# First casts of raw weights inside attention's slots: kept at their program place on ScalarE's queue

## The chip, the cores and the metric

The kernel runs on 1 core of a Trainium2 chip. The metric is device time in microseconds (us) of one execution, as the median of 3 runs. An execution was also taken by the hardware profiler; all lines in fences below come from it. TensorE (PE) does matmuls and transposes, VectorE (DVE) and ScalarE (ACT) do elementwise work, GpSimd (POOL) and SyncE (SP) issue transfers (DMAs). Each engine works through a queue of its own in a fixed order; semaphores tell it when another engine's result is there.

## The reference

One layer of a diffusion backbone over 512 latent tokens of width 1024, with 256 context tokens. Everything is in float32.

```python
h = _rmsnorm(x, pre_g) * (1 + sc) + sh            # sh, sc, gt from silu(c) @ w_mod + b_mod
parts = split_in(h @ w_in)                        # b, c, x_in, z_a, q, k, v, z_b, g_a, g_b: 10 x 1024 columns
q, k = rope(parts[4]), rope(parts[5]); v = parts[6]
attn = neighbourhood_attention(q, k, v, k_ctx, v_ctx, rpb)   # 8 x 16 window + all context keys, one softmax
y_a = (silu(z_a) * b * dwconv3(c * x_in, conv_w, conv_b)) @ w_out_conv
y_b = (silu(z_b) * attn) @ w_out_attn
y = (sigmoid(g_a) * y_a + sigmoid(g_b) * y_b) @ w_o
return x + gt * _rmsnorm(y, post_g)
```

## The kernel before

**Numbers as pairs.** A float32 matrix is multiplied as two fp32r parts, high H and low L: three matmuls (H by H, H by L, L by H) stand for one. The helper `split` (L64) makes the pair: ScalarE casts the source to H (L67), VectorE subtracts H from the source to get L (L70). So each weight passes once through ScalarE and at least once through VectorE before TensorE can use it.

**Chunks of weights.** `Chunk` (L83) is 256 columns of a weight matrix: two transfers of 512 KB into `raw` tiles (L89; three such buffers), first and second half of the contraction. A plain chunk goes through `split` (L91): one 128x1024 cast and subtraction per half. A chunk for `pair` (L294) is multiplied in 2 by 2 blocks with sums of blocks. `first` (L98) makes four weights of it in this order: cast B11 (L101), add on VectorE (L102), cast T1 (L103), cast B21 (L104), add (L105), cast T2 (L106), then two more adds. `second` (L114) makes T3, T4, B22 (and B12 for queries and keys) when the chunk is used. `pair` uses the four of `first` in its first half (L299 to L304, in the order B11, B21, T1, T2) and the others in its second half (L309 to L312); between the halves it calls `chunk.more()` (L307), which loads the next chunk. Between the products, ScalarE copies results out of PSUM (L300, L303, L305, L311), and VectorE adds into them (L306, L314, L317); a product can start only when the bank that it writes has been read out. Three banks serve these products inside attention (L843).

**Attention's slots.** The loop at L850 goes over 64 slots: 8 pairs of heads, 2 heads, 4 blocks of 128 queries. A slot does, in program order: some steps of other projections, listed in `plan` (L219) and run by `step(items)` (L859); at a head's first block the product with the values for the head before, `gather` (L862, matmuls at L773); the scores of the block two slots ahead, `scores` (L864: matmuls L717 or L726, bias and row minimum on VectorE L733, exponentials on ScalarE L740 and L744, division L745 and L747); and in every second slot `turn2` (L871): TensorE transposes two blocks of probabilities (L754) and `split` makes the pair TH, TL of them (L67 and L70 again).

**Where the raw casts stand.** `load` (L134) issues a chunk's transfers when a step asks for it. Inside the loop, `behind` is a list: `load` puts the chunk's `ready` (L142), that is its `first` or `split`, into it, and the slot runs the list at its very end (L872), behind `turn2`. So the casts of a chunk stand in the program at the end of the slot in which it was asked for. Outside the loop `behind` is None, and `ready` runs at once.

**Who orders a queue.** Only the start of the kernel (L432) has its order written out by hand. Elsewhere the framework that compiles the program orders each engine's queue: it runs the program against its own estimates of when inputs are there, and among the instructions that it takes for ready it issues the one that stands earliest in the program. An instruction whose inputs it takes for ready early is so put ahead of others that stand before it in the program. `tc.keep_in_program_order` adds an edge from the instruction before it in the program, on the same engine: it is queued behind that one. The edge is order alone: no semaphore and no instruction is added. `split` has the argument `pinned` for this; before the change only the keys of `keys_queries` use it (L685, L689).

Of the kernel before, what the change touches and what calls it, by code (L numbers as in the profile page):

```python
# [27 lines left out]
def layer(ctx: ExitStack, tc, xp, ctxt, ctxT, cc, wmod, small, wfirst, win, wout, wo, rel, tab, out):  # L28
# [35 lines left out]
    def split(H, L, src, scale=None, pinned=False):  # L64

        if scale is None:
            cast = nc.scalar.copy(H, src)  # L67
            if pinned:
                tc.keep_in_program_order(cast)
            nc.vector.tensor_sub(L, src, H.bitcast(F32))  # L70
        else:
            nc.scalar.mul(H, src, scale)
            nc.vector.scalar_tensor_tensor(
                out=L, in0=src, scalar=scale, in1=H.bitcast(F32), op0=ALU.mult, op1=ALU.subtract
            )
# [4 lines left out]
    def wtile(shape):  # L80
        return wp.tile(shape, F32R, name="w", bufs=4)

    class Chunk:  # L83
# [7 lines left out]
        def split(self):  # L91
            t = [wtile([P, 4, 2, 256]) for _ in range(2)]
            for x, raw in zip(t, self.raws):
                split(x[:, :, 0], x[:, :, 1], raw)
            k = range(KT)
            return tuple([t[i // 4][:, i % 4, y] for i in k] for y in range(2)) + ([t[i // 4][:, i % 4] for i in k],)

        def first(self, keep=False):  # L98
            (b11, b12), (b21, b22) = self.b = [(r[:, :, :P], r[:, :, P:]) for r in self.raws]
            t, sums = (wtile([P, 2, 2, 4, P]) for _ in range(2))  # L100
            split(t[:, 0, 0], t[:, 0, 1], b11)  # L101
            nc.vector.tensor_add(b11, b11, b12)  # L102
            split(sums[:, 0, 0], sums[:, 0, 1], b11)  # L103
            split(t[:, 1, 0], t[:, 1, 1], b21)  # L104
            nc.vector.tensor_add(b11, b11, b22)  # L105
            split(sums[:, 1, 0], sums[:, 1, 1], b11)  # L106
            self.keep = keep
            if not keep:
                nc.vector.tensor_add(b12, b12, b22)
            nc.vector.tensor_add(b21, b21, b11)  # L110
            self.B = {"B11": t[:, 0], "B21": t[:, 1], "T1": sums[:, 0], "T2": sums[:, 1]}
            return self
# [13 lines left out]
    behind = None  # L126
# [167 lines left out]
    def pair(c1, c2, w=None):  # L294

        w = w or chunk().B
        a, b, e = (pj()[:, :256] for _ in range(3))
        first, second = slice(0, 256), slice(256, S)
        product(a, A11, w["B11"], True)  # L299
        nc.scalar.copy(c1[:, first], a)  # L300
        product(b, A12, w["B21"], True)
        product(e, blocks_h["X1"], w["T1"], True)
        nc.scalar.copy(c2[:, second], e)  # L303
        product(a, blocks_h["S2"], w["T2"], False)  # L304
        nc.scalar.copy(c2[:, first], a)  # L305
        nc.vector.tensor_add(c1[:, first], c1[:, first], b)  # L306
        chunk.more()  # L307
        yield
        product(b, A22, w["T4"], True)  # L309
        product(a, blocks_h["S3"], w["T3"], False)  # L310
        nc.scalar.copy(c1[:, second], a)  # L311
        product(e, blocks_h["S4"], w["B22"], False)  # L312
        for cols, x in ((second, c1[:, second]), (first, e)):
            nc.vector.scalar_tensor_tensor(  # L314
                out=c2[:, cols], in0=c2[:, cols], scalar=-1.0, in1=x, op0=ALU.mult, op1=ALU.subtract
            )
        nc.vector.tensor_add(c1[:, second], c1[:, second], b)  # L317
# [388 lines left out]
    def scores(p, h, b):  # L706
# [31 lines left out]
        if b % 2 == 0:  # L738
            z = aw.tile([P, 2], F32, name="z", bufs=4)
            nc.scalar.activation(pt, s, AF.Exp, bias=m, scale=-1.0, accum_out=z[:, 0:1])  # L740
            whole[:] = pt, z
        else:
            first, z = whole
            nc.scalar.activation(pt, s, AF.Exp, bias=m, scale=-1.0, accum_out=z[:, 1:2])  # L744
            nc.vector.reciprocal(z, z)  # L745
            for i, x in enumerate((first, pt)):
                nc.scalar.mul(x, x, z[:, i:i + 1])  # L747
# [99 lines left out]
    behind = []  # L847
    sums = block_sums()
    done = 0
    for i, (p, h, b) in enumerate(blocks):  # L850
# [23 lines left out]
        behind = []  # L874
    behind = None
# [73 lines left out]
    for j in range(KT):  # L949
# [30 lines left out]
        if j == 4:  # L980
            A11, S3 = operand("A11", hp, ("u2", "u3")), operand("S3", hp, ("a2", "a3"))
            for q in range(2):
                split(A11[q][:, 0], A11[q][:, 1], raws[q][:, :, h0])
                x = cv.tile([P, S], F32, name="tb").rearrange("p (k c) -> p k c", k=2)
# [96 lines left out]
    t = [hp.tile([P, 2, S], F32R, name=f"wB22{i}", tag=f"h{2 + i}") for i in range(4)]  # L1081
# [122 lines left out]
```

## Time and profile before

| | |
|---|---|
| median of 3 runs | 709.12 us (709.09 to 709.35) |
| the profiled execution's own time | 709.01 us |
| its span, first to last instruction | 707.2 us |
| mean granted TensorE clock | 0.997 |
| PE busy | 695.0 us, 98% of the span |
| DVE busy | 586.3 us, 83% |
| ACT busy | 436.5 us, 62% |

The profiled execution's time is 1.8 us more than its span, and 0.11 us below the median. Lines of a timeline read: start in us from the span's start, length, engine, source line, operation, what is written from what, shape, count, and in brackets how long the engine had been idle and what ended that. Attention's loop lies at about 137 to 500 us. A line of a helper such as L67 or L70 serves many callers; the tile (`w<-raw` for weights, `TH<-ps` for probabilities) tells them apart.

### The profile page before, as it was taken

The numbers are of one execution on the slowest core, as the hardware profiler recorded it, in microseconds if no ns is written. First come the engines' busy times: TensorE is split into PE (matmuls) and PEld (weight loads), VectorE is DVE, ScalarE is ACT, GpSimd is POOL, SyncE is SP. The second block draws the span as 40 slices with busy tenths as digits, with TensorE's granted clock in tenths as the row PEclk, the third lists the DMA queues.
The fourth block names the chain that finished last, engine by engine and source line by source line (L and its number), as shares of the span: only waits on it lengthen the run. The fifth ranks groups of instructions, "written<-read, shape, count | busy, mean of one in ns | idle before, by whom it ended". The sixth has DMA issues, their size and how long they took to land.

```text
span 707.2 us, 11426 instructions
## 1 busy us (share of the span) xinstructions
PE 695.0 (98%) x4196; PEld 618.0 (87%) x4196; DVE 586.3 (83%) x1114; ACT 436.5 (62%) x868; POOL 66.9 (9%) x110
## 2 busy tenths in 40 slices
PE   7999999999999999999999999999999999999996
PEld 4888888888889989898999999999898899988885
DVE  6979997668599989978898797999799676665996
ACT  6566632656577677775876766778693444442563
POOL 0000002230130310301302203000000000000000
PEclk9999999999999999999999999999999999999998
DMA  8996896564351563542635436313733233560013
GB/s 338 406 354 227 284 339 173 131 164 144 99 105 24 135 176 116 127 138 60 168 106 165 103 125 157 101 61 105 247 117 116 87 120 120 198 250 30 31 59 120
DMA packets 37466, 108.27 MB, mean 153 GB/s; under 512 B 5025, under 2 KB 5281, under 8 KB 37410
## 3 DMA queue, kind: packets, MB, share of 16 engines
q1 hardware_dynamic: 28946, 92.20, 37.8%
q0 software_dynamic: 8320, 15.21, 10.7%
q8 instruction: 33, 0.54, 0.3%
q14 instruction: 23, 0.19, 0.1%
q10 hardware_dynamic: 144, 0.13, 0.1%
HBM read 87.07 MB, written 5.24 MB: 131 GB/s over the span
## 4 chain that ended last, share of the span: by engine, by line
PE 91%; DVE 4%; DMA 2%; ACT 1%; issue 1%; SPq 0%; POOL 0%; DVEq 0%; ACTq 0%
PE ps L289 25%; PE ps L164 11%; PE ps L166 11%; PE ps L165 11%; PE ps L177 6%; PE ps L1008 5%; PE ps L773 4%; PE ps L754 3%; PE ps L182 3%; PE ps L717 3%; PE ps L196 2%; PE ps L424 2%; PE ps L428 2%; PE ps L425 2%; DMA fraw<-in_wfirst 1%; PE ps L726 1%
## 5 line engine op out<-in xcount | busy, mean ns | idle before, releaser
L67 ACT CAST w<-raw 128x512 fp32r<-128x512 f32 (+1 forms) x193 | 137.3, 733 | 95.9 <-PE ps L166 31.3
L70 DVE TENSOR_TENSOR w<-raw,w 128x512 fp32r<-128x512 f32 (+1 forms) x193 | 156.6, 824 | 42.3 <-ACT w L67 40.9
L289 PE MATMUL ps<-S,w 128*128 128x256 f32 x960 | 121.9, 283 | 0.0
L289 PEld LDWEIGHTS ps<-S,w 128*128 128x128 f32 x960 | 118.2, 192 | 0.1
L289 PE MATMUL ps<-h,w 128*128 128x256 f32 x720 | 94.0, 284 | 0.6 <-DVE tc L306 0.5
L289 PEld LDWEIGHTS ps<-h,w 128*128 128x128 f32 x720 | 89.9, 191 | 2.5 <-DVE tc L306 0.7
L164 PE MATMUL ps<-h,w 128*128 128x512 f32 x208 | 81.5, 392 | 0.0
L166 PE MATMUL ps<-h,w 128*128 128x512 f32 x208 | 81.2, 390 | 0.0
L165 PE MATMUL ps<-h,w 128*128 128x512 f32 x208 | 81.0, 390 | 0.0
L626 POOL DMA_DIRECT2D tc<-tb x32 | 28.8, 1175 | 286.7 <-DVE tc L624 197.7
L747 ACT ACTIVATE pt<-pt,z 128x512 f32<-128x512 f32 x64 | 43.0, 724 | 6.0 <-DVE z L745 5.9
L166 PEld LDWEIGHTS ps<-h,w 128*128 128x128 f32 x208 | 39.0, 188 | 8.3
L165 PEld LDWEIGHTS ps<-h,w 128*128 128x128 f32 x208 | 39.1, 188 | 8.0
L164 PEld LDWEIGHTS ps<-h,w 128*128 128x128 f32 x208 | 39.1, 188 | 7.9
L67 ACT CAST TH<-ps 128x512 fp32r<-128x512 f32 x64 | 35.8, 589 | 15.5 <-PE ps L754 15.5
L733 DVE CUSTOM_DVE_ANT_1 ps<-ps,bt 128x512 f32<-128x512 f32 x56 | 38.8, 693 | 6.8 <-PE ps L717 6.5
L70 DVE TENSOR_TENSOR TL<-ps,TH 128x512 fp32r<-128x512 f32 x64 | 42.2, 682 | 1.0 <-ACT TH L67 0.7
L754 PE MATMUL ps<-ident,pt 128*128 128x128 f32 x256 | 33.3, 273 | 0.0
L177 PE MATMUL ps<-w,h 128*128 128x512 f32 x128 | 32.3, 394 | 0.0
L754 PEld LDWEIGHTS ps<-ident,pt 128*128 128x128 f32 x256 | 29.2, 140 | 2.1 <-ACT pt L747 0.2
L740 ACT ACTIVATE pt<-ps,m 128x512 f32<-128x512 f32 x32 | 22.0, 688 | 12.5 <-DVE m L733 11.8
L773 PE MATMUL ps<-TH,V 128*128 128x256 f32 (+1 forms) x96 | 28.5, 319 | 0.2 <-ACT TH L67 0.2
(249 smaller groups left out, 1387.8 us busy)
## 6 DMA issues: line engine op xcount, KB each, us to landing
raw<-in_win SPq DMA_DIRECT2D x74, 512.0 KB, 4.4
wm<-in_wmod SPq DMA_DIRECT2D x34, 512.0 KB, 6.4
raw<-in_wout SPq DMA_DIRECT2D x16, 512.0 KB, 3.6
bt<-in_rel SPq DMA_DIRECT2D x16, 256.0 KB, 2.9
tc<-tb POOLq DMA_DIRECT2D x32, 128.0 KB, 3.6
B<-in_wo SPq DMA_DIRECT2D x8, 512.0 KB, 6.4
fraw<-in_wfirst SPq DMA_DIRECT2D x8, 384.0 KB, 8.6
qd<-qd POOLq DMA_DIRECT2D x24, 128.0 KB, 2.3
```

What stands on the lines that cost most here:

```text
L67: cast = nc.scalar.copy(H, src)
L70: nc.vector.tensor_sub(L, src, H.bitcast(F32))
L164: nc.tensor.matmul(ps, lhsT=H[k][:, cs], rhs=mH[k], start=k == 0, stop=False)
L165: nc.tensor.matmul(ps, lhsT=H[k][:, cs], rhs=mL[k], start=False, stop=False)
L166: nc.tensor.matmul(ps, lhsT=L[k][:, cs], rhs=mH[k], start=False, stop=k == KT - 1)
L177: nc.tensor.matmul(ps, lhsT=mH[k][:, ts], rhs=both[k].rearrange("p a c -> p (a c)"), start=k == 0, stop=False, skip_group_check=True,)
L289: nc.tensor.matmul(ps, lhsT=w[:, x, k], rhs=act[y][k], start=start and k + o == 0, stop=k == 3 and o == 2, skip_group_check=True,)
L733: nc.vector.tensor_tensor_reduce(out=s3, in0=s3, in1=bt[:, e::4 - e][:, 0:2], scale=-1.0, scalar=3.0e38, op0=ALU.add, op1=ALU.min, accum_o ...
L747: nc.scalar.mul(x, x, z[:, i:i + 1])
L754: nc.tensor.transpose(tp[:, c], pt[:, c * P:(c + 1) * P], ident)
L773: nc.tensor.matmul(o3[:, dst], lhsT=V[p][:, kt, h], rhs=src(t), start=n == 0 and t is TH, stop=n == len(work) - 1 and t is TL,)
L1008: nc.tensor.matmul(out, lhsT=a(x, k, ts), rhs=w[y][k // 2][:, k % 2, cols], start=start and k + o == 0, stop=k == 3 and o == 2, skip_group ...
```

## The change

Three calls of `split` get `pinned`, true when `behind` is a list, that is inside attention's slots: the two casts of a plain chunk, and of a chunk for `pair` the casts of B11 and B21. The casts of sums (T1, T2) and those of `second` are not touched. A plain chunk's first cast then has its edge from whatever ScalarE instruction stands before it in the program (the end of the slot), its second cast from the first; B11's cast from the end of the slot, B21's from the cast of T1. Of the chunks asked for inside the loop, 14 are for `pair` and 9 are plain, so 46 casts get an edge. `split` itself (L64 to L75) stays as it is.

```diff
         def split(self):
             t = [wtile([P, 4, 2, 256]) for _ in range(2)]
             for x, raw in zip(t, self.raws):
-                split(x[:, :, 0], x[:, :, 1], raw)
+                split(x[:, :, 0], x[:, :, 1], raw, pinned=behind is not None)
...
             t, sums = (wtile([P, 2, 2, 4, P]) for _ in range(2))
-            split(t[:, 0, 0], t[:, 0, 1], b11)
+            split(t[:, 0, 0], t[:, 0, 1], b11, pinned=behind is not None)
             nc.vector.tensor_add(b11, b11, b12)
             split(sums[:, 0, 0], sums[:, 0, 1], b11)
-            split(t[:, 1, 0], t[:, 1, 1], b21)
+            split(t[:, 1, 0], t[:, 1, 1], b21, pinned=behind is not None)
```

## The prediction

> **What bounds the kernel now.** I read the page first, then the busy time by stretches of attention, then the timelines of PE, ACT and DVE where PE stands still, and last the chain of waits there. The page's first lines and the table by stretches (us, then PE, PEld, DVE, ACT, POOL busy with counts, granted clock, DMA share, GB/s):
>
> ```profile
> span 707.2 us, 11426 instructions
> PE 695.0 (98%) x4196; PEld 618.0 (87%) x4196; DVE 586.3 (83%) x1114; ACT 436.5 (62%) x868; POOL 66.9 (9%) x110
> ```
> ```profile
> 137.00:250.00 113.00, 113.00 (x669) 99.99 (x668) 93.18 (x203) 74.82 (x163) 22.27 (x34) 1.00 0.43 110
> 250.00:280.00 30.00, 28.82 (x221) 27.16 (x221) 28.11 (x58) 24.28 (x52) 2.57 (x5) 1.00 0.41 125
> 280.00:350.00 70.00, 70.00 (x467) 64.24 (x466) 57.73 (x126) 48.21 (x109) 16.52 (x26) 1.00 0.52 134
> 350.00:370.00 20.00, 20.00 (x162) 19.52 (x161) 19.65 (x42) 16.14 (x38) 0.00 (x0) 1.00 0.30 99
> 370.00:440.00 70.00, 70.00 (x462) 64.06 (x461) 58.36 (x127) 48.01 (x108) 16.00 (x25) 1.00 0.50 131
> 440.00:490.00 50.00, 50.00 (x398) 48.55 (x397) 48.98 (x102) 40.63 (x88) 0.51 (x1) 1.00 0.32 96
> ```
>
> TensorE is the bound: in attention it is busy throughout at full clock, but for one stretch, 250 to 280, with 1.18 us idle. VectorE comes close to being a second bound in 350 to 370 (19.65 of 20) and 440 to 490 (48.98 of 50). The change touches the order of attention alone, so what can be gained is what PE loses in that one stretch. PE's timeline there, and two undisturbed rows behind it for comparison:
>
> ```profile
> 247.04 1.04 PE L754 MATMUL ps<-ident,pt 128*128 128x128 f32 x8
> ...
> 249.35 3.04 PE L289 MATMUL ps<-S,w 128*128 128x256 f32 x24
> 252.55 0.49 PE L773 MATMUL ps<-TH,V 128*128 128x512 f32 x1 [0.16 <-ACT TH L67]
> 253.50 0.50 PE L773 MATMUL ps<-TL,V 128*128 128x512 f32 x1 [0.45 <-DVE TL L70]
> 253.83 0.40 PE L773 MATMUL ps<-TH,V 128*128 128x512 f32 x1
> 254.07 0.39 PE L773 MATMUL ps<-TL,V 128*128 128x512 f32 x1
> ...
> 258.57 3.04 PE L289 MATMUL ps<-S,w 128*128 128x256 f32 x24
> 261.45 0.40 PE L726 MATMUL ps<-ks,qd 128*128 128x256 f32 x2
> ...
> 261.93 1.03 PE L754 MATMUL ps<-ident,pt 128*128 128x128 f32 x8
> 263.44 1.69 PE L289 MATMUL ps<-h,w 128*128 128x256 f32 x12 [0.47 <-DVE tc L306]
> ...
> 269.57 3.46 PE L289 MATMUL ps<-h,w 128*128 128x256 f32 x24
> 272.87 3.04 PE L289 MATMUL ps<-S,w 128*128 128x256 f32 x24
> ...
> 282.87 1.04 PE L754 MATMUL ps<-ident,pt 128*128 128x128 f32 x8
> 283.66 0.70 PE L196 MATMUL ps<-hc,w 128*128 128x512 f32 x2
> ```
> ```profile
> 365.33 3.12 PE L289 MATMUL ps<-h,w 128*128 128x256 f32 x24
> 368.29 3.04 PE L289 MATMUL ps<-S,w 128*128 128x256 f32 x24
> ```
>
> Rows of PE overlap (253.50 + 0.50 is later than 253.83), so the loss is read from start to start. 24 matmuls take 2.88 (258.57 to 261.45), so `gather` was due at 249.35 + 2.88 = 252.23 and began 0.32 late. Its second matmul came 0.95 after the first and the third 0.33 after that, where 0.24 is usual (253.83 to 254.07): 0.71 and 0.09. Eight transposes are followed after 0.79 (282.87 to 283.66), here after 1.51: 0.72. The last 24 took 3.30, undisturbed ones in the same place 2.96 (365.33 to 368.29): 0.34. Together 2.18 us in three stalls: 1.12 at 252, 0.72 at 263, 0.34 at 271.
>
> The Trainium skill (Perfetto Trace Analysis, section Per-engine timelines) says that the end of a matmul is estimated from its size and not observed. By the idle time of the busy table all of it would be worth 1.18 us, 707.8; by the starts 2.18 us, 706.8. The overlapping rows agree with the page, so the starts count.
>
> The cause stands on ACT and DVE; the fourth fence is from the chain of waits, the last from the list of what casts of raw weights waited for in attention (us, times):
>
> ```profile
> 245.02 0.60 ACT L67 CAST w<-raw 128x512 fp32r<-128x512 f32 x1
> ...
> 250.24 0.62 ACT L67 CAST w<-raw 128x512 fp32r<-128x512 f32 x1 [3.08 <-DMA raw<-in_win]
> 250.76 0.58 ACT L67 CAST TH<-ps 128x512 fp32r<-128x512 f32 x1
> ...
> 251.91 0.59 ACT L67 CAST TH<-ps 128x512 fp32r<-128x512 f32 x1
> ```
> ```profile
> 250.89 0.69 DVE L70 TENSOR_TENSOR w<-raw,w 128x512 fp32r<-128x512 f32 x1 [2.19 <-ACT w L67]
> ```
> ```profile
> 262.98 0.41 DVE L306 TENSOR_TENSOR tc<-tc,ps 128x256 f32<-128x256 f32 x1
> ...
> 270.86 0.41 DVE L317 TENSOR_TENSOR tc<-tc,ps 128x256 f32<-128x256 f32 x1
> ```
> ```profile
> 244.39 5.82 DMA raw<-in_win
> ```
> ```profile
>   DMA raw<-in_win: 17.1, 14
> ```
>
> The casts at 245.02 and 250.24 are B11 and B21 of one chunk. In the program both stand behind `turn2`, whose TH casts are at 250.76 and 251.91: the framework put them ahead. B21's half was issued at 244.39 and landed at 250.21, and ScalarE stood 3.08 us in front of it, with the transposes of 247.04 done since about 247.83 and TH queued behind. VectorE, which subtracts B21 before TL, stood 2.19 us. Casts waited so 14 times in attention, 17.1 us in all, but only this wait reached PE.
>
> **The change part by part.** It adds no instruction and no wait; the same 46 casts run later. Three terms:
>
> 1. The stall at 252. With B11 behind TH and B21 behind T1's cast, TH can run from about 247.9, two casts of 0.58, done by 249.1; TL follows in VectorE's 2.19 idle us (248.70 to 250.89), done by about 250.4, well ahead of 252.23. Gain 1.12. The cast that waited is then B21's own, behind T1's: B11 at 249.1 puts T1's cast at about 251 or later, after the landing at 250.21, so the wait is gone and not moved. If the estimate for TH is off, the cover is 252.23 - 250.4 = 1.8 us.
>
> 2. The stalls at 263 and 271 are VectorE's backlog: between 250.89 and 262.98 its timeline has no idle bracket. With 2.19 less idle, L306 ends at 263.39 - 2.19 = 261.20; PE, 1.12 earlier, wants it at 262.72 - 1.12 = 261.60. Gain 0.72. L317 ends at 271.27 - 2.19 = 269.08, wanted at 271.33 - 0.34 - 1.84 = 269.15: no margin to speak of, so I take half of it, 0.17. Sum of gains 2.01.
>
> 3. The cost: weights come later. Lengths of one step, from the tile `raw` over the whole run (min/median/max in ns), and the tightest place I found, with ACT's rows:
>
> ```profile
> L67 ACT CAST w<-raw x193: 602/623/1065, 44.7 to 641.0; 128x512 fp32r<-128x512 f32 x143, 128x1024 fp32r<-128x1024 f32 x50
> L70 DVE TENSOR_TENSOR w<-raw,w x193: 666/687/1227, 45.8 to 642.4; 128x512 fp32r<-128x512 f32 x143, 128x1024 fp32r<-128x1024 f32 x50
> L102 DVE TENSOR_TENSOR raw<-raw x20: 664/686/693, 204.7 to 598.3; 128x512 f32<-128x512 f32 x20
> ```
> ```profile
> 355.27 0.62 ACT L67 CAST w<-raw 128x512 fp32r<-128x512 f32 x1 [0.37 <-PE ps L289]
> ...
> 360.22 1.09 ACT L67 CAST TH<-ps 128x512 fp32r<-128x512 f32 x2
> ...
> 369.21 0.36 ACT L300 COPY tc<-ps 128x256 f32<-128x256 f32 x1
> ```
>
> This chunk's B11 would move from 355.27 to behind TH, 360.22 + 1.09 = 361.31. B11 is whole one cast and one subtraction later, 361.31 + 0.62 + 0.69 = 362.62, and used at 365.33: 2.7 us spare. B21 (cast, subtract, add, T1's cast, its own cast and subtraction) 365.24, used half of 2.96 after 365.33, at 366.81: 1.6 spare. T2 (cast, subtract, add, cast, subtract, add, cast, subtract: 5.31) 366.62, used half of 2.88 after 368.29, at 369.73: 3.1 spare. So the weights' own chain fits. What may not fit is other work in VectorE's full queue between its steps. The bounds: nothing, where VectorE does the work that it now does later in the time made free (TH, TL and the row minimum come sooner by as much); at worst the second rival. A gain beyond 2.18 is excluded, since PE has no other stall in attention. I take 0.2, near the lower end, since the tightest spare time of 1.6 us still holds two other VectorE steps of 0.69. Plain chunks' `raw` buffers come free later by the same shift, which delays the next transfer on SP; the next casts are pinned later too, so that is covered. POOL's transfers keep their place.
>
> Sum: 709.01 - 2.01 + 0.20 = 707.2 us, against a profiled execution that lies 0.11 below the median of 709.12. A measurement of this kernel can tell about 0.2%, 1.4 us, from no change: faster is below 707.7, slower above 710.5.
>
> **The rivals.** First, *the gain is given back*: a pinned cast no longer stands before TH but before the next slot's copies, which PE needs as much. At 369.21 + 0.36 = 369.57 L300 frees the bank that PE writes at 369.73: 0.16 us spare. One cast of 0.62 in front makes 0.46 of stall; four such places among the 23 pinned chunks and sums give 1.84, with term 3 all 2.01. Time 709.0. The Trainium skill (Perfetto Trace Analysis, same section) calls ScalarE's queue strictly first in, first out, by which a wait can only be moved; the TH row directly behind the waiting cast agrees. Against the rival: most such copies are ready long before, and the transfers have landed by then.
>
> Second, *VectorE becomes the bound*, which ends slower. Where the framework now fills it with B11's subtraction and add ahead of TH, it would idle and pay later. That costs up to 2 x 0.69 = 1.38 us per pair chunk. In 440 to 490 four of them are made ready, by `plan` cx7, bz7 and the gates g0 and g1: 5.52 us, less VectorE's idle time left there, 50 - 48.98 = 1.02, and 0.16 spare at a bank as above: 4.34 for PE, less 2.01: 711.3. It decides once VectorE loses more than (2.01 + 1.02 + 0.16) / 4 = 0.8 us per chunk there. Against it: the row minimum, TH and TL move into that time.
>
> Third, *nothing moves*: the edge binds to one instruction, and where that floats ahead too, the cast follows. 709.0. The rows contradict it for B11 at 245.02, whose neighbour in the program ran at 251.91.
>
> **How the numbers follow.** Forecast 0.48 (own range 706.8 to 707.7), given back 0.32, VectorE 0.15, nothing 0.05. So faster 0.48, same 0.37, slower 0.15. The range runs from all 2.18 gained, 706.8, to 709.8, which takes in the middle cases with an overshoot of 0.8 and leaves out the second rival.
>
> **What would show it.** In the changed profile ACT's casts of `w<-raw` should wait for transfers well under 17.1 us, TH should come before B11 in the slot around 250, and PE's busy time in 250 to 280 should have no bracket. Brackets before L289 from L300, L305 or L306 elsewhere would show the first rival; brackets in 440 to 490 behind VectorE the second; an unchanged wait of about 3 us before a `w<-raw` cast at 250 would prove me wrong at term 1.

## The result and the profile after

The changed kernel takes 714.71 us (median of 6 runs), the kernel before on the same chip 709.24: ratio 1.0079, 95% interval 1.0065 to 1.0093. It is slower by 5.5 us where 1.9 us less was forecast. (One run of the kernel before, 763.03 us, was disturbed; without it the median before is 709.12, and the ratio rests on that.) The profiled execution took 714.84 us, 5.83 more than that of before.

The page's first lines:

```profile
span 713.0 us, 11421 instructions
...
PE 698.4 (98%) x4196; PEld 619.0 (87%) x4196; DVE 585.4 (82%) x1114; ACT 436.0 (61%) x868; POOL 66.8 (9%) x110
```

The stretches of the prediction's table, in its columns:

```profile
137.00:250.00 113.00, 111.77 (x646) 97.49 (x645) 89.89 (x195) 73.77 (x158) 20.14 (x30) 1.00 0.40 98
250.00:280.00 30.00, 27.96 (x218) 26.64 (x217) 27.40 (x58) 23.66 (x53) 4.66 (x9) 1.00 0.53 147
280.00:350.00 70.00, 69.81 (x462) 63.74 (x461) 57.48 (x126) 46.71 (x106) 14.93 (x23) 1.00 0.52 132
350.00:370.00 20.00, 20.00 (x160) 19.45 (x160) 18.64 (x39) 15.51 (x34) 1.55 (x3) 1.00 0.50 140
...
440.00:490.00 50.00, 49.41 (x389) 47.40 (x389) 46.20 (x98) 38.33 (x85) 3.21 (x7) 1.00 0.41 114
```

The work is the same, but TensorE now stands still in four of these five stretches. VectorE did less in all five (46.20 us in 440 to 490, where it did 48.98), in part because its work slipped into later stretches: it is not fuller in any of them. TensorE's timeline at the larger stalls:

```profile
206.78 1.11 PE L182 MATMUL ps<-w,h 128*128 128x256 f32 x8
208.43 0.50 PE L773 MATMUL ps<-TH,V 128*128 128x512 f32 x1 [0.54 <-ACT TH L67]
...
250.80 0.40 PE L717 MATMUL ps<-ks,qe 128*128 128x512 f32 x1
252.60 0.62 PE L289 MATMUL ps<-S,w 128*128 128x256 f32 x3 [1.41 <-ACT tc L303]
...
269.29 1.36 PE L289 MATMUL ps<-S,w 128*128 128x256 f32 x10
271.28 0.50 PE L717 MATMUL ps<-ks,qd 128*128 128x512 f32 x1 [0.64 <-DMA ks<-kl]
...
440.66 1.60 PE L289 MATMUL ps<-S,w 128*128 128x256 f32 x12
442.44 1.69 PE L289 MATMUL ps<-S,w 128*128 128x256 f32 x12 [0.18 <-ACT tc L300]
...
480.70 0.40 PE L717 MATMUL ps<-ks,qe 128*128 128x512 f32 x1
481.49 1.31 PE L289 MATMUL ps<-S,w 128*128 128x256 f32 x9 [0.40 <-DVE tc L314]
```

Read from start to start as in the prediction, the stalls of attention come to about 7.4 us: 1.5 at 208 (TH, then TL), 1.9 at 252, 0.9 at 271, 0.45 each at 346 and 442, 0.6 at 481, and a dozen of 0.1 to 0.4 at 167, 230, 487 and 506. Before there were 2.2, all between 252 and 272. The difference of 5.2 is nearly all of the 5.8 us by which the two profiled executions differ.

What ScalarE waited for in attention (us in total, times, longest), and VectorE's wait for the casts:

```profile
ACT pt L740 <- DVE m L733: 17.4, 18, 3.4
...
ACT ks L67 <- DMA tc<-tb: 7.6, 3, 4.8
```
```profile
DVE w L70 <- ACT w L67: 21.2, 20, 1.8
```

The waits for raw weights (17.1 us, 14 times before) are no longer in ScalarE's list, as forecast. In their place it waits 7.6 us for rope's transfers before casts of keys (1.8 before), and longer for VectorE's row minima (11.8 before). Rope's transfers (`tc<-tb`, L626) are those by which GpSimd finishes the rotation of queries and keys; their casts cannot run earlier. VectorE stands 21.2 us in front of casts of weights, 14.2 before. ScalarE's timeline at 204 and 251:

```profile
203.92 0.62 ACT L67 CAST ks<-tc 128x512 fp32r<-128x512 f32 x1 [2.57 <-DMA tc<-tb]
...
206.09 0.58 ACT L67 CAST TH<-ps 128x512 fp32r<-128x512 f32 x1
...
250.78 0.72 ACT L72 ACTIVATE qd<-tc 128x448 fp32r<-128x448 f32 x2 [1.78 <-DMA tc<-tb]
251.41 0.56 ACT L67 CAST TH<-ps 128x512 fp32r<-128x512 f32 x1
252.18 0.37 ACT L303 COPY tc<-ps 128x256 f32<-128x256 f32 x1 [0.21 <-DVE qe L73]
```

At 204 the kernel before had a raw cast in this place (200.56), and this cast of keys behind TH (205.40, without a wait). At 251 the queries' cast stood ahead of TH before too, but there rope let it start at 244.39, after a wait of 0.42.

A comparison of the queues' orders says why so much differs: 46 casts were pinned, but 165 instructions of ScalarE, 189 of VectorE and 115 of TensorE stand in another order (counted as those outside the longest common order). The framework ordered anew much that came behind the pins. So two questions are mixed in this profile: what the pins cost, and what the new order costs. The experiments part them.

### The profile page after: what moved, and what is told of

It reads as the page before. It is cut to its first block, busy times and chain, and to the rows that moved or that the text cites. A ratio compares the mean times of both kernels' runs of the same rounds, so it can differ in the third digit from the quotient of the medians.

```text
span 713.0 us, 11421 instructions
## 1 busy us (share of the span) xinstructions
PE 698.4 (98%) x4196; PEld 619.0 (87%) x4196; DVE 585.4 (82%) x1114; ACT 436.0 (61%) x868; POOL 66.8 (9%) x110
## 4 chain that ended last, share of the span: by engine, by line
PE 82%; DVE 6%; DMA 5%; ACT 3%; issue 2%; POOL 1%; DVEq 0%; SPq 0%; ACTq 0%
PE ps L289 23%; PE ps L164 10%; PE ps L165 10%; PE ps L166 9%; PE ps L177 6%; PE ps L1008 5%; PE ps L773 4%; DMA tc<-tb 3%; PE ps L182 3%; PE ps L754 3%; PE ps L717 3%; PE ps L424 2%; PE ps L428 2%; PE ps L425 2%; DVE w L70 1%
## 5 line engine op out<-in xcount | busy, mean ns | idle before, releaser
L70 DVE TENSOR_TENSOR w<-raw,w 128x512 fp32r<-128x512 f32 (+1 forms) x193 | 154.8, 824 | 48.4 <-ACT w L67 48.1
L67 ACT CAST w<-raw 128x512 fp32r<-128x512 f32 (+1 forms) x193 | 135.8, 731 | 82.5 <-PE ps L166 29.7
L289 PE MATMUL ps<-S,w 128*128 128x256 f32 x960 | 125.9, 284 | 2.2 <-ACT tc L303 1.4
L289 PEld LDWEIGHTS ps<-S,w 128*128 128x128 f32 x960 | 119.5, 192 | 3.8 <-ACT tc L303 1.8
L289 PE MATMUL ps<-h,w 128*128 128x256 f32 x720 | 94.3, 284 | 0.0
L289 PEld LDWEIGHTS ps<-h,w 128*128 128x128 f32 x720 | 90.2, 191 | 1.4
L626 POOL DMA_DIRECT2D tc<-tb x32 | 28.6, 1168 | 296.4 <-DVE tc L624 199.2
L733 DVE CUSTOM_DVE_ANT_1 ps<-ps,bt 128x512 f32<-128x512 f32 x56 | 38.7, 694 | 7.1 <-PE ps L717 6.7
L70 DVE TENSOR_TENSOR TL<-ps,TH 128x512 fp32r<-128x512 f32 x64 | 42.1, 682 | 2.7 <-ACT TH L67 2.6
L773 PE MATMUL ps<-TH,V 128*128 128x256 f32 (+1 forms) x96 | 28.7, 320 | 0.5 <-ACT TH L67 0.5
```

What stands on the lines that cost most here:

```text
L289: nc.tensor.matmul(ps, lhsT=w[:, x, k], rhs=act[y][k], start=start and k + o == 0, stop=k == 3 and o == 2, skip_group_check=True,)
L733: nc.vector.tensor_tensor_reduce(out=s3, in0=s3, in1=bt[:, e::4 - e][:, 0:2], scale=-1.0, scalar=3.0e38, op0=ALU.add, op1=ALU.min, accum_o ...
L773: nc.tensor.matmul(o3[:, dst], lhsT=V[p][:, kt, h], rhs=src(t), start=n == 0 and t is TH, stop=n == len(work) - 1 and t is TL,)
```

## The experiments

Theory A: other casts, which wait for rope's transfers, took the free places at the head of ScalarE's queue. Theory B: the weights' sums come too late and stand in VectorE's way. Theory C: the new order of the rest is at fault, not the pins. Each time is compared with runs of the kernel before on the same chip. The expectations name single chunks as `plan` does (qk2, qk3, cx5).

| run | pins | the rest | us | before | ratio, 95% interval |
|---|---|---|---|---|---|
| e1 | all 46 | held | 727.10 | 709.05 | 1.0236 to 1.0267 |
| e2 | all, and rope's casts | free | 710.09 | 709.05 | 1.0010 to 1.0029 |
| e3 | B11, B21 | free | 712.16 | 709.05 | 1.0035 to 1.0065 |
| e4 | plain chunks | free | 709.04 | 709.05 | 0.9991 to 1.0010 |
| e5 | all, keys' cast moved | held as after | 715.07 | 708.89 | 1.0075 to 1.0105 |
| e6 | B21 of cx5 | free | 706.98 | 708.89 | 0.9963 to 0.9983 |
| e7 | B21 | free | 706.72 | 708.89 | 0.9960 to 0.9982 |
| e8 | B11 | held | 719.89 | 708.89 | 1.0137 to 1.0171 |
| e9 | B21, plain chunks | free | 707.14 | 708.69 | 0.9969 to 0.9987 |
| e10 | B11 | free | 713.53 | 708.69 | 1.0047 to 1.0083 |
| e11 | all, keys' cast and TL moved | held as after | 712.17 | 708.69 | 1.0036 to 1.0066 |
| e12 | B21 | held | 707.87 | 708.69 | 0.9977 to 0.9997 |
| e13 | B11 of qk3 | held | 710.93 | 709.22 | 1.0015 to 1.0034 |
| e14 | B11, VectorE relieved | held | 718.13 | 709.22 | 1.0113 to 1.0147 |
| e15 | none, VectorE relieved | held | 708.54 | 709.22 | 0.9981 to 1.0000 |

### The pins without the new order

The order of a kernel can be held by edges of the same kind as the pins, between each instruction and the one that stood before it on its engine. Only what `first`, `split` and `second` of the chunks inside attention issue is left free:

```diff
+def hold(tc, free):
...
+                if mine[k].name in free:
+                    continue
+                if prev is not None:
+                    tc.add_manual_dep(
+                        mine[k], prev.name,
+                        mybir.DependencyInfo(mybir.DependencyClass.NoSync, mybir.DependencyReason.DATA),
+                        reason="hold",
+                    )
+                prev = mine[k]
```

> The same 46 pins, but every instruction that does not belong to the preparation of weights keeps, on each of the five engines, the place that it has in the kernel before (edges without a wait); only the casts, subtractions and sums of the chunks of attention are free to move. Theory A (other casts, which depend on rope's transfers, took the free places at the head of ScalarE's queue) and theory C (the framework ordered the rest anew, and that is what costs): the stalls at 208 and at 252 are not there, 707.0 to 709.5 us. Theory B (the weights themselves come too late, and stand before copies and row minima when they come): the stalls at 346, 442 and 481 to 506 stay, and those at 230 to 260 that come from late sums, at least 712 us.

Measured 727.10: 18 us slower. Theory C falls: with the rest held, which is the case that the prediction worked out, the pins cost more than three times as much, so the new order gave most of it back. Theory B was right in sign; "at least 712" said nothing of the size, and the time lies 15 us above it. (About 1.6 us of it are slow matmuls behind a stall at 230; the last section has them.)

### Which pins

Each of the three sets alone, then two together, by leaving `pinned` out of the other calls:

```diff
-            split(t[:, 0, 0], t[:, 0, 1], b11, pinned=behind is not None)
+            split(t[:, 0, 0], t[:, 0, 1], b11, pinned=False)
```

> Only the 18 casts of the plain chunks pinned. TensorE's order is that of the kernel before, and the pair chunks' first casts stay ahead, so the cast of keys stays behind TH at 204 and the wait for B21 at 250 stays too. Theories A and B: within 0.5 us of the kernel before, 708.7 to 709.7. Theory C: small too, since 48 of 786 ScalarE instructions move and none of TensorE's: 708.5 to 710.5.

709.04, no change; the stalls at 252 to 272 are those of before.

> Only the 28 casts of the pair chunks pinned, not the 18 of the plain chunks. Around 204 and 251 ScalarE's order is that of the changed kernel. Theory A: the stalls at 208 and 252 stay, 713.5 to 714.8 us. Theory B: the same, since the sums are in pair chunks. Theory C: more than 100 of TensorE's instructions stand in another order here too, 712 to 716.

712.16, below the 713.5 of theories A and B and just within theory C's range. The stalls at 208 (1.3 us) and 251 (0.7) are there, smaller than in the changed kernel.

> Only B21's casts pinned (14), B11's and the plain chunks' free. Theory B (what costs is that the sums of a pair chunk start late on VectorE, which B11 decides): near the kernel before or better, 707.2 to 709.5 us. Theory A: B11 stays in its place at 200.56, so the cast of keys stays behind TH at 204: no stall at 208; 707.2 to 709.5 as well. If the pins of B21 alone explain the loss: 712 or more.

706.72: faster than both kernels, by 2.17 us.

> Only B11's 14 pins, all else free as in the changed kernel. Theory B11: the loss is here alone, 712 to 716 us, and the wait of B21's cast may be gone by itself, since its place follows the sums. Theory A: ScalarE's order at 204 has the cast of keys behind TH here, so the stall at 208 is not there; those at 230 to 270 and behind 340 are. If the loss needs B21's pins as well: 709 to 711.

713.53. The loss is here, without a stall at 208. The largest are 2.0 at 251, behind a queries' cast that waits for rope with VectorE's subtraction for `qe` behind it, and 1.2 at 363, behind three subtractions of weights on VectorE. Theory A foresaw no stall at 208 here too, so this run alone does not part it from theory B; the held runs below do.

> The changed kernel without B11's 14 pins: B21's casts and the plain chunks' stay pinned. Theory B11 (the whole loss hangs on B11's pins; B21's give the gain; the plain chunks' do nothing): 706.5 to 707.5 us, with no stall of note in attention, against 706.7 with B21's alone. If the three parts do not add up, because each set makes the framework order the rest anew: 708 to 713.

707.14: the changed kernel without B11's pins has the gain.

One pin alone, that of the cast which waited 3.08 us (n is the chunk's number in the order of loading, handed to it for this):

```diff
-            split(t[:, 1, 0], t[:, 1, 1], b21, pinned=behind is not None)
+            split(t[:, 1, 0], t[:, 1, 1], b21, pinned=self.n == 17)
```

> One pin alone: B21's cast of cx5, which waited 3.08 us for its transfer at 250 in the kernel before. TensorE's order is that of the kernel before, 12 casts of ScalarE and 12 instructions of VectorE stand elsewhere, all around 250. Term 1 of the prediction: gather at 252 starts without its 1.12 us, and what follows on VectorE at 263 and 271 shrinks as well, 707.0 to 708.0 us. If the wait only changes its place: 708.8 to 709.4. If the later subtraction costs VectorE more than the wait did: above 709.4.

706.98, 1.91 us faster. One pin does nearly all that fourteen do. TensorE's timeline with all of B21's pins, in the stretch of the prediction's three stalls, and ScalarE's there:

```profile
249.20 3.04 PE L289 MATMUL ps<-S,w 128*128 128x256 f32 x24
252.08 0.40 PE L773 MATMUL ps<-TH,V 128*128 128x512 f32 x1
...
260.64 1.03 PE L754 MATMUL ps<-ident,pt 128*128 128x128 f32 x8
261.43 1.67 PE L289 MATMUL ps<-h,w 128*128 128x256 f32 x12
...
267.54 3.18 PE L289 MATMUL ps<-h,w 128*128 128x256 f32 x24
270.56 3.04 PE L289 MATMUL ps<-S,w 128*128 128x256 f32 x24
```
```profile
247.53 1.07 ACT L67 CAST TH<-ps 128x512 fp32r<-128x512 f32 x2 [0.53 <-PE ps L754]
...
249.39 1.13 ACT L67 CAST w<-raw 128x512 fp32r<-128x512 f32 x2
```

No bracket on TensorE is left. `gather` follows its 24 matmuls after 2.88, the transposes are followed after 0.79, the last 24 take 3.02. TH waits for TensorE alone, and B21's cast runs behind T1's, both without a wait. No idle bracket is left in attention, so another order of these casts can hardly gain more there.

### Why B11's pins cost

First the two halves with the rest held:

> As in the first run of these, everything but the weights' preparation is held in the order of the kernel before, and only B11's casts are pinned (14), so that no rope cast and no other instruction can change its place against the rest. Theory B: the sums that hang on B11 (two subtractions, two additions and two more behind T1 and T2, 0.69 us each) fall into the time in which VectorE has row minima and copies to do, so most of the 18 us of the first run are here as well: 718 to 727 us. If the plain chunks and B21 made the loss of the first run: below 714.

> Everything but the weights' preparation held in the order of the kernel before, B21's 14 casts pinned. It is the counterpart of the run that held the rest and pinned B11 (719.9): if holding the rest is what costs there, this one is slow as well, above 712; if it is B11's pins, this one is like B21's pins without holding, 706.5 to 707.5 us.

719.89 and 707.87 (a little above its range). It is B11, and not the holding. What TensorE waited for in the first of the two (the lines of the held kernels lie 103 to 110 higher: L317 is L208, L398 is L289, L415 is L306; below, L173 is L70, L206 and L209 are the adds L102 and L105, L843 is L733, L883 is L773):

```profile
PE ps L398 <- DVE ta L317: 2.6, 3, 1.3
PE ps L398 <- DVE tc L415: 2.5, 3, 1.7
```

These are banks that VectorE has not read out yet. The list names no weight. Then one chunk alone:

```diff
-            split(t[:, 0, 0], t[:, 0, 1], b11, pinned=behind is not None)
+            split(t[:, 0, 0], t[:, 0, 1], b11, pinned=self.n == 15)
```

> The rest held in the order of the kernel before, and B11's cast of one chunk alone pinned, that of qk3 (200.56 in the kernel before). 5 instructions of ScalarE and 7 of VectorE stand elsewhere. If B11's pins cost by the chunk, through VectorE: the stall at 228 to 231 of the run with all of B11's pins (1.7 us) is here, and nothing else but the stall at 252 of the kernel before: 710.0 to 711.0 us. If it takes several pinned chunks, one behind the other, to make VectorE late: 708.5 to 709.3.

710.93, 1.71 us more, by 5 and 7 moved instructions. VectorE's timeline in the kernel before, and then with the one pin:

```profile
203.18 0.67 DVE L70 TENSOR_TENSOR w<-raw,w 128x512 fp32r<-128x512 f32 x1
...
204.70 0.69 DVE L102 TENSOR_TENSOR raw<-raw 128x512 f32<-128x512 f32 x1
...
211.02 0.67 DVE L105 TENSOR_TENSOR raw<-raw 128x512 f32<-128x512 f32 x1
...
212.22 0.68 DVE L110 TENSOR_TENSOR raw<-raw 128x512 f32<-128x512 f32 x1
212.82 0.68 DVE L70 TENSOR_TENSOR w<-raw,w 128x512 fp32r<-128x512 f32 x1
...
216.30 0.69 DVE L733 CUSTOM_DVE_ANT_0 ps<-ps,bt 128x512 f32<-128x512 f32 x1
...
226.55 1.28 DVE L70 TENSOR_TENSOR TL<-ps,TH 128x512 fp32r<-128x512 f32 x2
```
```profile
203.25 0.67 DVE L173 TENSOR_TENSOR w<-raw,w 128x512 fp32r<-128x512 f32 x1
...
212.29 0.68 DVE L173 TENSOR_TENSOR w<-raw,w 128x512 fp32r<-128x512 f32 x1
...
213.38 0.68 DVE L206 TENSOR_TENSOR raw<-raw 128x512 f32<-128x512 f32 x1
...
215.59 0.68 DVE L209 TENSOR_TENSOR raw<-raw 128x512 f32<-128x512 f32 x1
...
217.43 0.69 DVE L173 TENSOR_TENSOR w<-raw,w 128x512 fp32r<-128x512 f32 x1
...
218.37 0.69 DVE L843 CUSTOM_DVE_ANT_0 ps<-ps,bt 128x512 f32<-128x512 f32 x1
...
228.36 1.28 DVE L173 TENSOR_TENSOR TL<-ps,TH 128x512 fp32r<-128x512 f32 x2
```

In the kernel before the chain runs from 203.18 to 213.5, one step here and there between other work; two of its steps lie in 212 to 218. With the pin it begins at 212.29 (only B21's free subtraction takes the early place) and six of its steps lie in 212 to 218. The row minimum behind them moves from 216.30 to 218.37, the subtractions for TL, which stand further back in the same queue, from 226.55 to 228.36. VectorE's busy time (the third figure behind the length of the stretch) shows the same, in the kernel before and then with the one pin: 1.68 us of it have left the first stretch, and the second is all but full.

```profile
195.00:212.00 17.00, 17.00 (x104) 15.06 (x103) 15.83 (x39) 13.62 (x32) 6.56 (x11) 1.00 0.51 107
212.00:232.00 20.00, 20.00 (x139) 18.47 (x139) 19.05 (x45) 15.50 (x39) 0.00 (x0) 1.00 0.19 49
```
```profile
195.00:212.00 17.00, 17.00 (x103) 15.02 (x103) 14.15 (x36) 12.89 (x30) 6.54 (x11) 1.00 0.49 103
212.00:232.00 20.00, 18.98 (x128) 16.92 (x127) 19.68 (x47) 15.01 (x37) 0.00 (x0) 1.00 0.13 31
```

TensorE's timeline in this run:

```profile
228.40 0.50 PE L883 MATMUL ps<-TH,V 128*128 128x512 f32 x1
229.70 0.49 PE L883 MATMUL ps<-TL,V 128*128 128x512 f32 x1 [0.80 <-DVE TL L173]
```

The second matmul comes 1.30 after the first, where 0.23 is usual; with 0.17 ahead and 0.46 behind that is the 1.7 us.

Last, VectorE relieved of other work up to 230, with every instruction in its place. These two kernels leave out the block sums, so the casts made from them no longer wait for VectorE either:

```diff
-                nc.vector.tensor_add(x, hx[0][i].bitcast(F32), hx[1][i].bitcast(F32))
+                nc.vector.tensor_add(x[:, :8], hx[0][i][:, :8].bitcast(F32), hx[1][i][:, :8].bitcast(F32))
...
+            a, b = hx[0][k].bitcast(F32), hx[0][4 + k].bitcast(F32)
```

> The run with the rest held and B11's 14 casts pinned (719.9), with VectorE relieved up to 230: the sums of the blocks of h (24 VectorE instructions in the first two pairs of heads, 0.4 to 0.7 us each) are made over 4 or 8 columns, and S2 to X1 are cast from h itself, so this kernel leaves the block sums out. Their places in the queues, and all else, stay. If VectorE's time is what B11's pins cost: the stall at 228 to 231 (1.7 us) is gone, those behind 240, where nothing is relieved, stay: 716.5 to 718.4 us. If the weights come too late for TensorE or ScalarE's order is at fault: 719.5 to 720.5.

> The kernel before in its own order with the same relief of VectorE (the block sums left out), as the other end of the comparison: TensorE has no stall up to 250 there, so 708.2 to 709.0 us by all theories.

718.13 and 708.54. Against the kernel before on the same chip the loss is 8.9 us instead of 11.0 in the one case, 2.1 less; in the other the relief alone gains 0.7, at the edge of no change. The total came as expected, the place only in part. Against the run without relief the row minimum lies at 217.58 instead of 218.31, TL at 227.57 instead of 228.30, and the stall shrinks from 1.7 to 1.0 us and does not go. The rest of the 2.1 lies in that 0.7 and at later stalls that are larger in the profiled execution without relief, which was the longest of its four (721.49). So dose and answer agree at 228 (0.73 us of VectorE, 0.7 of TensorE); the total proves less than it seems.

### What the new order adds

> The changed kernel, and also the casts that wait for rope's transfers (keys of the plain chunks, all queries) pinned to their place in the program. Theory A: the cast of keys that stood before TH at 204 goes behind it, so the stall of 1.5 us at 208 is gone; the queries' cast at 251 stands before TH in the program as well, so the stall at 252 stays: about 713.2 us. Theory B: nothing of the weights changes, 714.7 us. Theory C: the framework orders the rest anew once more, so the stalls lie in other places than in the changed kernel and the time can be anywhere from 711 to 717.

```diff
-            keys(k, slice(0, S), blocks)
+            keys(k, slice(0, S), True)
...
-                split(qd[0][:, dst], qe[0][:, dst], q[:, src], 0.125)
+                split(qd[0][:, dst], qe[0][:, dst], q[:, src], 0.125, pinned=True)
```

710.09, 1.0 us more than the kernel before instead of 5.5: a larger gain than expected. The stalls at 208 and 252 are both gone, though the queries' cast kept its place ahead of TH: rope came earlier there (246.79, after a wait of 0.29). As these pins order the rest anew too, a cleaner test holds the order of the changed kernel and moves the one cast of keys behind TH:

```diff
+            cast = keys(k, slice(0, S), blocks)
+            if p == 2:
...
+                tc.add_manual_dep(
+                    cast.ins, behind_th[0].ins.name,
```

> The changed kernel with every engine's order held as it is, except for one instruction: the cast of the keys of qk2 (203.92, 2.57 us of wait for rope's transfer) goes from its place ahead of the exponentials and TH to where the kernel before has it, behind TH and the copy at 208.26; its subtraction on VectorE follows it. Theory A: the stall of 1.5 us at 208 is gone, and VectorE, which ran 2.5 us later in the changed kernel from there on, has the sums and the rope of the next pair ready earlier, so the stall of 1.6 us at 252 shrinks too: 711.6 to 713.3 us, of which 1.5 is the direct part. Theory B (late weights, full VectorE): only the direct part or less, 713.2 to 714.7 us, with the stall at 252 as it was.

715.07, a miss for theory A's sum, and above theory B's as well. The cast moved, TH ran at 203.43, but the stall only changed its engine:

```profile
206.54 0.69 DVE L179 TENSOR_TENSOR kl<-tc,ks 128x512 fp32r<-128x512 f32 x1 [2.49 <-ACT ks L176]
```
```profile
210.01 0.50 PE L890 MATMUL ps<-TL,V 128*128 128x512 f32 x1 [2.18 <-DVE TL L179]
```

VectorE's queue still had the keys' subtraction ahead of TL's, and stood in front of it. So TL's two subtractions went ahead as well:

> The run with the keys' cast moved once more, but on VectorE as well: the two subtractions for TL go ahead of the keys' subtraction, which in that run stood 2.49 us for the cast with TL behind it. One instruction of ScalarE and three of VectorE stand elsewhere than in the changed kernel. Theory A: TH and TL are done by 206.5, so the stall at 208 to 210 is gone (1.5 us), and VectorE is less late at 252: 711.8 to 713.3 us. If the loss there is not from the keys' cast: 714.5 or more.

712.17. The stall at 208 to 210 is gone, that at 252 shrinks from 1.6 to 0.6, and 1.1 us of new ones come at 222 to 224. Against the kernel before on the same chip the loss is 3.5 us and not 5.5: one cast of ScalarE and three subtractions of VectorE are worth 2 us. That is theory A at one place, shown; for the places at 271 and 442 it is only read from the profile.

## Why the prediction was wrong

**Terms 1 and 2 were right, in mechanism and size.** Forecast 2.01 us, cap 2.18; B21's pin of cx5 alone gave 1.91, all of B21's 2.17. TH was done at 248.60, forecast by 249.1, and the stalls at 263 and 271 went with the one at 252, as VectorE's backlog. B21's place alone decided: B11's cast stayed ahead, at 245.06 in the run with one pin. In the changed kernel itself the gain cannot be seen, since other waits stand at 252 and 271.

**Term 3 failed**: "What may not fit is other work in VectorE's full queue between its steps ... I take 0.2, near the lower end". The lower end rested on VectorE doing "the work that it now does later in the time made free". It could not: row minima, TH and TL depend on TensorE's results and came no sooner, so the time freed stayed in part idle (VectorE worked 14.15 us in 195 to 212 with one pin, 14.21 with all of B11's, 15.83 before) and the steps piled up at 212 to 218. The row minimum was 2.07 us late for one chunk, and TensorE lost 1.7. With all of B11's pins and the rest held it is 11.0 us, or 0.8 per chunk, 14 times; the term stood for all of them at 0.2. In the changed kernel it comes to about 7.6 us: the 5.5 lost and the 2.2 that B21's pins alone gain, with the cost of the new order in it. Spare time was checked for the weights' own chain (1.6 us at the tightest place), and that chain did fit: TensorE hardly waits for weights. What had to be checked was the spare time of what stands behind the chain on VectorE.

**The premise failed too**: "the same 46 casts run later". Ten times as many instructions changed places. That moved the loss from 18 us (held) to 5.5, and put rope-bound casts in front of TH and bank copies, 2 us of it at one cast of keys. The prediction knew that the framework orders by its own estimates, and reckoned without it.

**The rivals.** The second, VectorE as the bound, was the right one; its place (440 to 490) was wrong, and its chance (0.15) too low. The table's first stretch, 137 to 250 with VectorE busy 93.18 of 113 us, hid a full one: 19.05 of 20 in 212 to 232, where the first pair chunk's steps came to lie. In 440 to 490 only 0.6 us were lost behind VectorE, at 481. The first is there in small: TensorE waits 0.45 us each at 346 and 442 for L300's copies. That a wait in such a queue can only be moved did not hold: with B21's pins alone ScalarE waits 6.1 us for raw weights instead of 17.1, and no bracket on TensorE came in place of those at 252 and 263. The third is excluded. The measured time lies above the range (709.8 at most) and on the other side of the kernel before.

**What stays open.** In the held order B11's and B21's pins give 11.0 and -0.8 us, all three sets 18.1; of the missing 7.9, about 1.6 are the slow matmuls named below, and the rest was not taken apart. In the changed kernel's own order only the one cast of keys was moved in a run; the stalls at 252, 271, 346 and 442 are read from the profile. In the free order the sets do not add up either: 4.8, -2.2 and 0.0 against 5.5.

## What to carry to other kernels

Where an early cast fills idle time on a second engine, its place is worth what that engine would otherwise do there: before moving a step later, follow everything that hangs on it on every queue, and check the spare time of what stands behind it, not only of the step itself. Pin the one instruction whose wait is seen to reach the bound (here one cast, 1.9 us), not its whole family. Where a framework orders the queues, an order edge can re-order much that follows; to learn what the edge itself does, hold the rest.

## What the hardware showed unexpectedly

A stall of TensorE can cost more than its length. In the run with the keys' cast moved, TensorE stood 2.18 us before the matmul at 210.01, and the granted clock (third column from the right) then fell to half:

```profile
210.00:212.00 2.00, 1.99 (x10) 1.85 (x11) 2.00 (x6) 1.19 (x6) 0.19 (x1) 0.76 0.59 128
212.00:214.00 2.00, 2.00 (x7) 1.64 (x7) 2.00 (x7) 0.74 (x2) 0.00 (x0) 0.50 0.00 0
214.00:216.00 2.00, 2.00 (x11) 1.65 (x10) 1.90 (x6) 1.29 (x3) 0.00 (x0) 0.88 0.00 0
```

From start to start that adds about 1.6 us of slow matmuls to the 2.35 of the stall, so this run says less against theory A than its time does. The same happened in the run with all 46 pins and the rest held, behind three shorter waits close together: 0.61, 0.80 and 0.21 us before the matmuls at 228.66, 229.96 and 230.67, in all 2.3 us from start to start. The granted clock was then 0.73, 0.50 and 0.92 in the three stretches of 2 us from 230 on, again about 1.6 us of slow matmuls. Single waits of 1.41 (252 in the changed kernel), 1.77 (251 with B11's pins alone) and 1.93 us (249 in that held run) left the clock at 1.00, so the length of the longest wait does not tell; what does is not shown. The Trainium skill (TensorE: Matmul & The Clock Gate, Part 1) gives an idle window of about 3.4 us for this. Here 2.18 us in one wait was enough, and 1.62 in three.
